# A two-layer hybrid step: small-block products of the scan in two rounds, layer norm chunk by chunk, tensor work from GpSimd to VectorE

## The chip, the core and the metric

One core of a Trainium2 chip. The metric is the device time of one execution in microseconds (us). Before the change the median of three runs is 2641.58 us (2641.39 to 2647.34). The profiler took one more execution, which is the one all rows below come from.

## What is computed

One step of a two-layer network on 256 tokens of width 2048: 128 prompt tokens (called g = 0 in the kernel) and 128 sample tokens (g = 1). Cut to the parts around the change:

```python
def hybrid_layer(x, mods, ...):          # once for prompt, once for sample; 2 layers
    shift1, scale1, gate1, shift2, scale2, gate2 = mods      # silu(c) @ w_mod + b_mod
    h = x * (1 + scale1) + shift1
    q, k, v, hq, hff, hfb, hi, hgt = split_in(h @ w_in)      # 2048 x 6656
    att = rms_norm(attend(q, k, v, sink), attn_g)
    hg, s_f, s_b = hgrn_mixer(hq, hff, hfb, hi, hgt, ...)    # two scans, forward and backward
    mix = concatenate([att, hg], -1) @ w_o
    x = layer_norm(ALPHA * x + gate1 * mix, ln_g[0], ln_b[0])
    ffn = square(relu((x * (1 + scale2) + shift2) @ w_up)) @ w_down   # 2048 x 8192 x 2048
    x = layer_norm(ALPHA * x + gate2 * ffn, ln_g[1], ln_b[1])

def hgrn_chunk_scan(q, k, v, log_f, s0):     # chunks of 32 tokens, 8 heads
    # inside a chunk: a = tril(q~ k~^T), o = a v
    # across chunks: s <- exp(sum log_f) * s + u;  o += (q exp(b)) s
```

## The kernel before

**Weights.** All large weights (w_in, w_o, w_up, w_down and the modulation weights w_mod) come from HBM as half tiles of 128x1024 (512 KB) into ten buffers `raw`, issued on SyncE's queue whenever a buffer is free. A 512x512 piece of a large weight is a main item. Its two halves are split into a rounded part `wh` (cast on ScalarE, L1324) and a rest `wl` (subtraction on VectorE, L1325), four buffers each, which is one main item ahead of TensorE. The activations are split in the same way (`hh`, `hl` and the like: L408 on ScalarE, L409 on VectorE). There are 392 main items. In a unit of kind T the weights are the stationary operand and the 256 tokens stream (48 matmuls of 256 columns: L436, L438, L439). In a unit of kind N the tokens are stationary and the weights stream (24 matmuls of 512 columns: L448, L449, L450), into one accumulator `acc` for each of the two groups of tokens; there are three such PSUM banks. Each item runs its k in two halves, both groups of tokens in each half.

**Modulation.** A piece of w_mod goes either to TensorE as 2-column matmuls into `psm` (L203, L223: the stationary operand is 2 columns wide, in a narrow column tile of the array) or to VectorE (`ma`, L266).

**Tasks around the mains.** Scans, attention, stores and the tail of a layer norm are generators; `between()` and a step after each main item advance them by up to a yield. So what a generator emits between two yields lands together in the stream of an engine. GpSimd and SyncE run in program order, TensorE, VectorE and ScalarE in the order that a scheduler makes of the program.

**The scan.** For two heads and both groups of tokens (m = 0..3) a scan works on four chunks of 32 tokens. The products inside a chunk go to `pI` (L748). The products across chunks go to `pX` in three rounds, one per later chunk: 4 matmuls with all 128 columns of `kd` stationary and 32 columns of `qb` streaming (L777), between them VectorE multiplies the earlier chunks of `kd` by decays; then a masked copy with masks `fx`, `bx` on VectorE takes `pX` over into `aT`. There are 16 such scans, eight per layer.

**End of a unit and of a stage.** A finished accumulator is taken over by VectorE: in w_o by `add_gated` (L887 multiplies by the gate, L890 or L892 adds to `Y`), in w_down by L1236 (adds to `Z`) or, in the last round, L1240 and L1241. The gate tiles `G` (128x512, two buffers) are loaded from DRAM by GpSimd's queue (L876) and the same two buffers serve the layer norm's scale and shift rows (L998, L999). `pre_sum` (L1224, L1225) multiplies `Z` by the gate.

**Layer norm.** After the last unit of w_o (and of w_down in the first layer) `ln_head` normalises all eight 128x512 tiles on VectorE (L909), then `ln_mod` transposes four chunks n by TensorE (L931), applies scale and shift (g = 0: two VectorE operations over 128x512, L934 and L936; g = 1: four ScalarE operations, L940) and splits. `ln_out` applies the norm's own scale and shift for the residual (L1002, L1003 on GpSimd) and runs as a task beside the next stage's mains.

## Time and profile before

| | us |
|---|---|
| median of 3 runs | 2641.58 |
| the profiled execution, its own time | 2641.68 |
| its span in the trace | 2639.9 |
| TensorE busy | 2536.6 (96%) |
| VectorE busy | 1862.5 (71%) |
| ScalarE busy | 1214.5 (46%) |
| GpSimd busy | 230.9 (9%) |
| mean rate of all transfers | 247 GB/s |

TensorE's busy time is a modelled one: matmuls overlap, and each record ends later than the next one starts. So 96% does not say that 4% is left; what TensorE loses is read from the distance of one start to the next, and from the waits. The stages by time: first layer's w_in to about 500, its w_o to 617, its MLP to about 1400, second layer's w_in to about 1800, its w_o to 1880, its MLP to 2618, and the last layer norm's tail to the end.

### The profile page before, as it was taken

The numbers are of one execution on the slowest core, as the hardware profiler recorded it, in microseconds if no ns is written. First come the engines' busy times: TensorE is split into PE (matmuls) and PEld (weight loads), VectorE is DVE, ScalarE is ACT, GpSimd is POOL, SyncE is SP. The second block draws the span as 40 slices with busy tenths as digits, with TensorE's granted clock in tenths as the row PEclk, the third lists the DMA queues.
The fourth block names the chain that finished last, engine by engine and source line by source line (L and its number), as shares of the span: only waits on it lengthen the run. The fifth ranks groups of instructions, "written<-read, shape, count | busy, mean of one in ns | idle before, by whom it ended". The sixth has DMA issues, their size and how long they took to land.

```text
span 2639.9 us, 41114 instructions
## 1 busy us (share of the span) xinstructions
PE 2536.6 (96%) x16276; PEld 2178.1 (83%) x16276; DVE 1862.5 (71%) x2290; ACT 1214.5 (46%) x1655; POOL 230.9 (9%) x266
## 2 busy tenths in 40 slices
PE   7999999998999999999999999999799999999996
PEld 4787777756988979979887989888798998998985
DVE  3455777658887777887778888877865565656656
ACT  3434554434444533534434656644454454443442
POOL 2000000014100000000014100001420000000003
PEclk9999999999999999999999999999899999999998
DMA  9889778868887878787879556566566666666663
GB/s 359 287 283 324 265 244 273 297 231 323 281 307 276 276 261 287 265 281 258 287 251 331 195 191 204 177 228 212 186 225 208 222 202 227 212 207 225 205 206 115
DMA packets 192369, 652.91 MB, mean 247 GB/s; under 512 B 22752, under 2 KB 25376, under 8 KB 192176
## 3 DMA queue, kind: packets, MB, share of 16 engines
q1 hardware_dynamic: 177680, 614.56, 68.0%
q0 software_dynamic: 11552, 33.04, 4.4%
q8 instruction: 127, 2.08, 0.3%
q10 hardware_dynamic: 2944, 2.69, 0.3%
q14 instruction: 66, 0.54, 0.1%
HBM read 643.32 MB, written 6.88 MB: 246 GB/s over the span
## 4 chain that ended last, share of the span: by engine, by line
PE 76%; DMA 10%; DVE 9%; issue 3%; ACT 1%; SPq 0%; POOL 0%; DVEq 0%; ACTq 0%; POOLq 0%
PE acc L436 12%; PE acc L439 12%; PE acc L438 12%; PE acc L448 11%; PE acc L449 11%; PE acc L450 11%; DMA raw<-in_w_mod_dram 6%; DVE wl L1325 3%; DVE ma L266 2%; PE psm L203 2%; PE pX L777 1%; DMA raw<-in_w_up_dram 1%; DMA raw<-in_w_in_dram 1%; PE psm L223 1%; DMA out_nsf_dram<-lf 1%
## 5 line engine op out<-in xcount | busy, mean ns | idle before, releaser
L1324 ACT CAST wh<-raw 128x1024 fp32r<-128x1024 f32 x784 | 821.8, 1049 | 1140.3 <-PE acc L450 489.0
L1325 DVE TENSOR_TENSOR wl<-raw,wh 128x1024 fp32r<-128x1024 f32 x784 | 971.2, 1246 | 433.3 <-ACT wh L1324 406.6
L436 PE MATMUL acc<-hh,wh 128*128 128x256 f32 x3072 | 875.9, 285 | 3.4 <-DVE q L599 1.9
L439 PE MATMUL acc<-hh,wl 128*128 128x256 f32 x3072 | 870.5, 284 | 7.9 <-DVE wl L1325 7.7
L438 PE MATMUL acc<-hl,wh 128*128 128x256 f32 x3072 | 869.7, 283 | 1.2 <-DVE hl L409 1.2
L436 PEld LDWEIGHTS acc<-hh,wh 128*128 128x128 f32 x3072 | 589.0, 192 | 39.2 <-issue 26.0
L439 PEld LDWEIGHTS acc<-hh,wl 128*128 128x128 f32 x3072 | 588.6, 192 | 11.2 <-DVE wl L1325 10.4
L438 PEld LDWEIGHTS acc<-hl,wh 128*128 128x128 f32 x3072 | 589.0, 192 | 2.9 <-DVE hl L409 2.2
L266 DVE SCALAR_TENSOR_TENSOR ma<-raw,stat,ma 128x1024 f32<-128x1024 f32 x300 | 388.5, 1313 | 113.4 <-DMA raw<-in_w_mod_dram 111.8
L448 PE MATMUL acc<-wh,fh 128*128 128x512 f32 x1024 | 401.8, 392 | 7.0 <-DVE Z L1236 6.8
L449 PE MATMUL acc<-wl,fh 128*128 128x512 f32 x1024 | 400.4, 391 | 0.4 <-DVE wl L1325 0.4
L450 PE MATMUL acc<-wh,fl 128*128 128x512 f32 x1024 | 399.7, 390 | 0.0
L448 PEld LDWEIGHTS acc<-wh,fh 128*128 128x128 f32 x1024 | 193.0, 188 | 57.8 <-DVE Z L1236 8.1
L449 PEld LDWEIGHTS acc<-wl,fh 128*128 128x128 f32 x1024 | 193.0, 188 | 40.8 <-DVE wl L1325 1.5
L450 PEld LDWEIGHTS acc<-wh,fl 128*128 128x128 f32 x1024 | 193.1, 189 | 40.4
L448 PE MATMUL acc<-wh,hh 128*128 128x512 f32 x320 | 129.5, 406 | 3.0 <-ACT hh L408 2.4
L449 PE MATMUL acc<-wl,hh 128*128 128x512 f32 x320 | 127.5, 398 | 0.3 <-DVE wl L1325 0.3
L450 PE MATMUL acc<-wh,hl 128*128 128x512 f32 x320 | 125.9, 394 | 1.9 <-DVE hl L409 1.9
L448 PE MATMUL acc<-wh,mxh 128*128 128x512 f32 x256 | 105.0, 411 | 5.9 <-DVE G L887 5.3
L876 POOL DMA_DIRECT2D G<-gr x48 | 26.3, 548 | 953.2 <-DVE Z L1241 408.9
L203 PE MATMUL psm<-raw,stat 128*2 128x512 f32 x640 | 96.6, 598 | 8.1 <-DMA raw<-in_w_mod_dram 8.1
L450 PE MATMUL acc<-wh,mxl 128*128 128x512 f32 x256 | 101.5, 398 | 0.0
(366 smaller groups left out, 2124.6 us busy)
## 6 DMA issues: line engine op xcount, KB each, us to landing
raw<-in_w_mod_dram SPq DMA_DIRECT2D x384, 512.0 KB
raw<-in_w_up_dram SPq DMA_DIRECT2D x256, 512.0 KB
raw<-in_w_down_dram SPq DMA_DIRECT2D x256, 512.0 KB
raw<-in_w_in_dram SPq DMA_DIRECT2D x208, 512.0 KB
raw<-in_w_o_dram SPq DMA_DIRECT2D x64, 512.0 KB
G<-gr POOLq DMA_DIRECT2D x48, 256.0 KB, 5.1
G<-in_lng_dram POOLq DMA_DIRECT2D x12, 256.0 KB, 5.8
G<-in_lnb_dram POOLq DMA_DIRECT2D x12, 256.0 KB, 7.1
```

The source lines that it names most:

```text
L203: pe.matmul(self.ps[32 * j:32 * j + 2, :], lhsT=stat[:, k, :], rhs=raw[j // 2][:, 512 * (j % 2):512 * (j % 2) + 512], start=k == 0, stop=k ...
L223: pe.matmul(self.ps[32 * j:32 * j + 2, :], lhsT=stat[:, 4 * k + j, :], rhs=raw[j // 2][:, 512 * (j % 2):512 * (j % 2) + 512], start=k == 0 ...
L266: dve.scalar_tensor_tensor(self.acc[g], raw[h], c, self.acc[g], ALU.mult, ALU.add)
L436: pe.matmul(ps, lhsT=w0, rhs=hi[:, k], start=f and k == 0 and m % 2 == 0, stop=False, skip_group_check=True)
L438: pe.matmul(ps, lhsT=w0, rhs=lo[:, k], start=False, stop=False, skip_group_check=True)
L439: pe.matmul(ps, lhsT=w1, rhs=hi[:, k], start=False, stop=e and k == 3 and m % 2 == 1, skip_group_check=True)
L448: pe.matmul(ps, lhsT=hi[:, k, gs], rhs=wh[k], start=f and k == 0, stop=False)
L449: pe.matmul(ps, lhsT=hi[:, k, gs], rhs=wl[k], start=False, stop=False)
L450: pe.matmul(ps, lhsT=lo[:, k, gs], rhs=wh[k], start=False, stop=e and k == 3)
L777: pe.matmul(pX[:, 128 * m + 32 * c:128 * m + 32 * c + 32], lhsT=kd[:, 128 * m:128 * m + 128], rhs=qb[:, 128 * m + 32 * c:128 * m + 32 * c ...
L1324: act.copy(wh, r)
L1325: dve.tensor_tensor(wl, r, wh.bitcast(F32), ALU.subtract)
```

## The change

1. In the last item of each N unit, the 12 matmuls of g = 0 come first, then `between()`, then those of g = 1 (`n_tile`).
2. The scan's products across chunks take two rounds: first two blocks of 32x32 for each m (8 matmuls, 32 stationary columns), then one of 64x64 (4 matmuls, 64 stationary columns), each at the column tile of the array where its rows lie. Three ScalarE copies take them over; the masks `fx` and `bx`, their loads and casts go.
3. `ln_head` goes; `ln_mod` normalises two tiles for each chunk n, then transposes, g = 1 first. `scale_shift` does g = 0 by four VectorE operations over 128x128; the first layer's input uses it too.
4. The additions of `add_gated` (12), the multiplications of `pre_sum` (16) and both operations of `ln_out` (48) move from GpSimd to VectorE: 76 operations over 128x512.
5. `ln_out` is spread by yields: 24 ahead of it, 6 behind each pair of loads, 3 behind each tile.

```diff
-        for key in ("fi", "bi", "fx", "bx"):
+        for key in ("fi", "bi"):
...
+        if un.kind == "N" and e:
+            for g in range(2):
+                if g == 1:
+                    between()
+                n_tile(un, g, range(4), hi, lo, wh, wl, f, e)
+            return
...
+    def n_tile(un, g, ks, hi, lo, wh, wl, f, e):
+        if f and ks[0] == 0:
+            un.ps[g] = accp.tile([128, 512], F32, tag="acc", name=nm("acc"))
+        ps = un.ps[g]
+        gs = slice(128 * g, 128 * g + 128)
+        for k in ks:
+            pe.matmul(ps, lhsT=hi[:, k, gs], rhs=wh[k], start=f and k == 0, stop=False)
+            pe.matmul(ps, lhsT=hi[:, k, gs], rhs=wl[k], start=False, stop=False)
+            pe.matmul(ps, lhsT=lo[:, k, gs], rhs=wh[k], start=False, stop=e and k == 3)
...
-        order = [0, 1, 2, 3] if fwd else [3, 2, 1, 0]
+        c0, c1, c2, c3 = order = [0, 1, 2, 3] if fwd else [3, 2, 1, 0]
+
+        early, late = slice(min(c0, c1), max(c0, c1) + 1), slice(min(c2, c3), max(c2, c3) + 1)
+        cols = lambda m, sl: slice(128 * m + 32 * sl.start, 128 * m + 32 * sl.stop)
+        rows = lambda sl: slice(32 * sl.start, 32 * sl.stop)
+        one = lambda c: slice(c, c + 1)
         pX = bank("pX")
+
+        def across(ss, ts):
+            for m in range(4):
+                pe.matmul(pX[rows(ss), cols(m, ts)], lhsT=kd[:, cols(m, ss)], rhs=qb[:, cols(m, ts)],
+                          start=True, stop=True, tile_position=(0, 32 * ss.start))
+
+        across(one(c0), one(c1))
+        across(one(c2), one(c3))
...
-        for i in range(1, 4):
-            c = order[i]
-            pc = order[:i]
-            if i >= 2:
-                sl = slice(min(pc[:-1]), max(pc[:-1]) + 1)
-                n = i - 1
-                d = dm[:, :, pc[-1]:pc[-1] + 1].unsqueeze(3).to_broadcast([128, 4, n, 32])
-                kk = kdv[:, :, sl, :]
-                flat = lambda x: x.rearrange("p m c t -> p m (c t)")
-                dve.tensor_tensor(flat(kk), flat(kk),
-                                  dm[:, :, pc[-1]:pc[-1] + 1].to_broadcast([128, 4, n * 32]), ALU.mult)
-            for m in range(4):
-                pe.matmul(pX[:, 128 * m + 32 * c:128 * m + 32 * c + 32], lhsT=kd[:, 128 * m:128 * m + 128],
-                          rhs=qb[:, 128 * m + 32 * c:128 * m + 32 * c + 32], start=True, stop=True)
-            if i == 1:
-                cum = small(8).rearrange("p (h c) -> p h c", h=2)
-                for hl in range(2):
-                    m = 2 * hl + 1
-                    dve.memset(cum[:, hl, order[0]:order[0] + 1], 1.0)
-                    for x in range(1, 4):
-                        pcol, ccol = order[x - 1], order[x]
-                        dve.tensor_tensor(cum[:, hl, ccol:ccol + 1], cum[:, hl, pcol:pcol + 1],
-                                          dm[:, m, pcol:pcol + 1], ALU.mult)
-                for hl in range(2):
-                    dve.tensor_tensor(
-                        qS[:, 128 * hl:128 * hl + 128].rearrange("p (c t) -> p c t", c=4),
-                        qbv[:, 2 * hl + 1], cum[:, hl, :].unsqueeze(2).to_broadcast([128, 4, 32]), ALU.mult)
-            yield
-        cs = slice(32 * min(order[1:]), 32 * max(order[1:]) + 32)
-        dve.copy_predicated(v3(aT, 4)[:, :, cs],
-                            masks[mk + "x"][:, cs].unsqueeze(1).to_broadcast([128, 4, 96]),
-                            v3(pX, 4)[:, :, cs])
-        pc = order[:3]
-        lc = order[3]
-        for m in (0, 2):
-            sl = slice(128 * m + 32 * min(pc), 128 * m + 32 * max(pc) + 32)
-            dve.tensor_scalar(kd[:, sl], kd[:, sl], dm[:, m, lc:lc + 1], None, ALU.mult)
+        cum = small(8).rearrange("p (h c) -> p h c", h=2)
+        do = dm[:, 1::2]
+        dve.memset(cum[:, :, c0:c0 + 1], 1.0)
+        for x in range(1, 4):
+            pc, cc = order[x - 1], order[x]
+            dve.tensor_tensor(cum[:, :, cc:cc + 1], cum[:, :, pc:pc + 1], do[:, :, pc:pc + 1], ALU.mult)
+        for hl in range(2):
+            dve.tensor_tensor(qS[:, 128 * hl:128 * hl + 128].rearrange("p (c t) -> p c t", c=4),
+                              qbv[:, 2 * hl + 1], cum[:, hl, :].unsqueeze(2).to_broadcast([128, 4, 32]), ALU.mult)
+        yield
+        dve.tensor_tensor(kdv[:, :, c0], kdv[:, :, c0], dm[:, :, c1:c1 + 1].to_broadcast([128, 4, 32]), ALU.mult)
+        dve.tensor_tensor(qbv[:, :, c3], qbv[:, :, c3], dm[:, :, c2:c2 + 1].to_broadcast([128, 4, 32]), ALU.mult)
+        across(early, late)
+        yield
+        aTv = v3(aT, 4)
+        for ss, ts in ((one(c0), one(c1)), (one(c2), one(c3)), (early, late)):
+            act.copy(aTv[rows(ss), :, rows(ts)], v3(pX, 4)[rows(ss), :, rows(ts)])
+
+        de = small(2).unsqueeze(2)
+        dg = dm[:, 0::2]
+        kg = kdv[:, 0::2]
+        dve.tensor_tensor(de, dg[:, :, c2:c2 + 1], dg[:, :, c3:c3 + 1], ALU.mult)
+        flat = lambda x: x.rearrange("p m c t -> p m (c t)")
+        dve.tensor_tensor(flat(kg[:, :, early]), flat(kg[:, :, early]), de.to_broadcast([128, 2, 64]), ALU.mult)
+        dve.tensor_tensor(kg[:, :, c2], kg[:, :, c2], dg[:, :, c3:c3 + 1].to_broadcast([128, 2, 32]), ALU.mult)
...
-            (dve if n == 3 else pool).tensor_tensor(y, y, t, ALU.add)
+            dve.tensor_tensor(y, y, t, ALU.add)
...
-    def ln_head(key):
-        mr = ln_stat(key)
-        for n in range(4):
-            for g in range(2):
-                y = yt[key, n, g]
-                dve.tensor_scalar(y, y, mr[g][0], mr[g][1], ALU.subtract, ALU.mult)
...
+    def scale_shift(out, src, A, B, g):
+
+        for c in range(4):
+            o_, s_ = (x[:, 128 * c:128 * c + 128] for x in (out, src))
+            if g == 0:
+                dve.tensor_scalar(o_, s_, A[:, c, g:g + 1], B[:, c, g:g + 1], ALU.mult, ALU.add)
+            else:
+                act.activation(o_, s_, AF.Identity, scale=A[:, c, g:g + 1], bias=B[:, c, g:g + 1])
+
     def ln_mod(key, AB, dst):
 
         A, B = AB
+        mr = ln_stat(key)
         for n in range(4):
             hl = new_act("h")
-            for g in range(2):
+            fs = slice(4 * n, 4 * n + 4)
+            for g in (1, 0):
+                y = yt[key, n, g]
+                dve.tensor_scalar(y, y, mr[g][0], mr[g][1], ALU.subtract, ALU.mult)
+            for g in (1, 0):
                 y = yt[key, n, g]
                 pt = bank("pt")
                 for c in range(4):
                     pe.transpose(pt[:, 128 * c:128 * c + 128], y[:, 128 * c:128 * c + 128], K["ident"])
                 t = u("ed")
-                if g == 0:
-                    dve.tensor_tensor(v3(t, 4), v3(pt, 4),
-                                      A[:, 4 * n:4 * n + 4, g:g + 1].to_broadcast([128, 4, 128]), ALU.mult)
-                    dve.tensor_tensor(v3(t, 4), v3(t, 4),
-                                      B[:, 4 * n:4 * n + 4, g:g + 1].to_broadcast([128, 4, 128]), ALU.add)
-                else:
-                    for c in range(4):
-                        act.activation(t[:, 128 * c:128 * c + 128], pt[:, 128 * c:128 * c + 128], AF.Identity,
-                                       scale=A[:, 4 * n + c, g:g + 1], bias=B[:, 4 * n + c, g:g + 1])
+                scale_shift(t, pt, A[:, fs], B[:, fs], g)
...
-        tag = "G"
+        for _ in range(24):
+            yield
         for n in range(4):
-            gt, bt = u(tag), u(tag)
+            gt, bt = u("G"), u("G")
             side.dma_start(gt, a["lng"][li:li + 1, 512 * n:512 * n + 512].partition_broadcast(128))
             side.dma_start(bt, a["lnb"][li:li + 1, 512 * n:512 * n + 512].partition_broadcast(128))
+            for _ in range(6):
+                yield
             for g in range(2):
                 y = yt.pop((key, n, g))
-                pool.tensor_tensor(y, y, gt, ALU.mult)
-                pool.tensor_tensor(y, y, bt, ALU.add)
+                dve.tensor_tensor(y, y, gt, ALU.mult)
+                dve.tensor_tensor(y, y, bt, ALU.add)
                 sink_fn(n, g, y)
-            yield
+                for _ in range(3):
+                    yield
...
-                    pool.tensor_tensor(t, t, gch[l, 5, n, g, 0], ALU.mult)
+                    dve.tensor_tensor(t, t, gch[l, 5, n, g, 0], ALU.mult)
```

In the changed kernel the lines are shifted: L777 is L780, L448 to L450 are L457 to L459, L1236 is L1241, L1325 is L1329, `ln_out`'s operations are L1013 and L1014.

The order of instructions on TensorE at the first layer's first two scans, before (`t` and `ed` are the scan's `kd` and `qb`):

```order
L450 MATMUL acc_2698<-wh_2686,hl_2037 128x512
L448 MATMUL acc_2705<-wh_2686,hh_2036 128x512
L777 MATMUL pX_2642<-t_2489,ed_2532 128x32 x4
L777 MATMUL pX_2662<-t_2498,ed_2544 128x32 x4
L449 MATMUL acc_2705<-wl_2687,hh_2036 128x512
L450 MATMUL acc_2705<-wh_2686,hl_2037 128x512
L777 MATMUL pX_2642<-t_2489,ed_2532 128x32 x4
L777 MATMUL pX_2662<-t_2498,ed_2544 128x32 x4
```

And after, the first round of the first scan:

```order
L458 MATMUL acc_2698<-wl_2563,hh_2020 128x512
L459 MATMUL acc_2698<-wh_2562,hl_2021 128x512
L780 MATMUL pX_2642<-t_2489,ed_2532 32x32 x8
L457 MATMUL acc_2705<-wh_2562,hh_2020 128x512
L458 MATMUL acc_2705<-wl_2563,hh_2020 128x512
```

and its second round, at the same weights as before (`wh_2686`, and the item's second half `wh_2690`):

```order
L458 MATMUL acc_2698<-wl_2687,hh_2034 128x512
L459 MATMUL acc_2698<-wh_2686,hl_2035 128x512
L457 MATMUL acc_2698<-wh_2690,hh_2034 128x512
L458 MATMUL acc_2698<-wl_2691,hh_2034 128x512
L459 MATMUL acc_2698<-wh_2690,hl_2035 128x512
L780 MATMUL pX_2642<-t_2489,ed_2532 64x64 x4
L780 MATMUL pX_2662<-t_2498,ed_2544 64x64 x4
L457 MATMUL acc_2698<-wh_2690,hh_2034 128x512
L458 MATMUL acc_2698<-wl_2691,hh_2034 128x512
```

Three rounds of `128x32 x4` for each scan have become one `32x32 x8` and one `64x64 x4`. The last rows also show the new order in a unit's last item: `acc_2698` goes on to the second half of the weights, where before `acc_2705` had its turn.

On VectorE, at the end of a w_down unit in the first MLP, before (`Z` is the running sum over units, `ma` the modulation sum):

```order
L266 SCALAR_TENSOR_TENSOR ma_9071<-raw_9369,stat,ma_9071 128x1024
L266 SCALAR_TENSOR_TENSOR ma_9072<-raw_9369,stat,ma_9072 128x1024
L1236 TENSOR_TENSOR Z_7610<-Z_7610,acc_9257 128x512
L1236 TENSOR_TENSOR Z_7612<-Z_7612,acc_9264 128x512
L1325 TENSOR_TENSOR wl_9410<-raw_9299,wh_9409 128x1024
```

And after, at the end of the same unit (the tiles' numbers are shifted, 7610 to 7614):

```order
L1329 TENSOR_TENSOR wl_9384<-raw_9263,wh_9383 128x1024
L1241 TENSOR_TENSOR Z_7614<-Z_7614,acc_9265 128x512
L266 SCALAR_TENSOR_TENSOR ma_9079<-raw_9377,stat,ma_9079 128x1024
L266 SCALAR_TENSOR_TENSOR ma_9080<-raw_9377,stat,ma_9080 128x1024
L1241 TENSOR_TENSOR Z_7616<-Z_7616,acc_9272 128x512
L1329 TENSOR_TENSOR wl_9418<-raw_9307,wh_9417 128x1024
```

The two additions that free the accumulators stood together behind the modulation's operations; now they stand apart, the first directly behind the split `wl`.

On GpSimd, at the start of the second layer's MLP, before:

```order
L998 DMA G_18015<-in_lng_dram 128x512
L999 DMA G_18016<-in_lnb_dram 128x512
L1002 TENSOR_TENSOR Y_17008<-Y_17008,G_18015 128x512
L1003 TENSOR_TENSOR Y_17008<-Y_17008,G_18016 128x512
L1002 TENSOR_TENSOR Y_17012<-Y_17012,G_18015 128x512
L1003 TENSOR_TENSOR Y_17012<-Y_17012,G_18016 128x512
L998 DMA G_18061<-in_lng_dram 128x512
L999 DMA G_18062<-in_lnb_dram 128x512
```

And on VectorE in the changed kernel, for the same tiles `Y`:

```order
L409 TENSOR_TENSOR hl_18012<-ed_18032,hh_18011 128x4x128
L1013 TENSOR_TENSOR Y_17024<-Y_17024,G_18819 128x512
L1013 TENSOR_TENSOR Y_17028<-Y_17028,G_18819 128x512
L1329 TENSOR_TENSOR wl_18176<-raw_17839,wh_18175 128x1024
L1014 TENSOR_TENSOR Y_17024<-Y_17024,G_18820 128x512
L1014 TENSOR_TENSOR Y_17028<-Y_17028,G_18820 128x512
L1013 TENSOR_TENSOR Y_17151<-Y_17151,G_19163 128x512
L1329 TENSOR_TENSOR wl_18232<-raw_17875,wh_18231 128x1024
L1013 TENSOR_TENSOR Y_17155<-Y_17155,G_19163 128x512
L1014 TENSOR_TENSOR Y_17151<-Y_17151,G_19164 128x512
L1329 TENSOR_TENSOR wl_18236<-raw_17877,wh_18235 128x1024
L1014 TENSOR_TENSOR Y_17155<-Y_17155,G_19164 128x512
```

GpSimd waited by itself for the reloads of `G` between these operations; now they stand in VectorE's stream, between the splits `wl`, and the second pair of loads (`G_19163`, `G_19164`) uses the buffers of the first (`G_18819`, `G_18820`).

## Rows read from the trace of the kernel before

**Rows 1.** The page, part 1: busy us (share of the span) and instructions of each engine.

```profile
PE 2536.6 (96%) x16276; PEld 2178.1 (83%) x16276; DVE 1862.5 (71%) x2290; ACT 1214.5 (46%) x1655; POOL 230.9 (9%) x266
```

**Rows 2.** Windows: length, busy PE, PEld, DVE, ACT, POOL, PEclk, DMA share, GB/s.

```profile
254.00:500.00 246.00, 236.71 (x1623) 186.04 (x1616) 183.57 (x371) 123.70 (x227) 14.83 (x28) 0.99 0.77 261
...
620.00:1390.00 770.00, 754.58 (x4817) 664.39 (x4816) 617.87 (x566) 352.62 (x402) 52.65 (x46) 1.00 0.81 277
...
1420.00:1850.00 430.00, 420.18 (x2841) 379.60 (x2840) 342.36 (x552) 239.24 (x400) 47.19 (x62) 1.00 0.63 208
...
1930.00:2618.00 688.00, 687.52 (x4358) 625.33 (x4358) 412.08 (x377) 309.14 (x341) 22.61 (x31) 1.00 0.63 208
```

**Rows 3.** Single lines: duration ns min/median/max, first and last start, form.

```profile
L777 PEld LDWEIGHTS pX<-t,ed x192: 187/192/192, 279.7 to 1651.6; 128*128 128x128 f32 x192
L777 PE MATMUL pX<-t,ed x192: 190/276/276, 279.9 to 1651.6; 128*128 128x32 f32 x192
L275 PEld LDWEIGHTS ph<-ma,ones x80: 106/108/109, 740.3 to 2529.9; 128*32 128x32 f32 x80
```

**Rows 4.** Timeline: start us, us from first start to last end, record, count.

```profile
30.88 1.05 PE L233 MATMUL pt<-sel,w 128*128 128x2 f32 x8 [0.69 <-ACT w L230]
...
289.12 1.87 PE L777 MATMUL pX<-t,ed 128*128 128x32 f32 x16
```

**Rows 5.** Timeline at a change from 128 stationary columns to 2 and back.

```profile
929.14 0.39 PE L450 MATMUL acc<-wh,fl 128*128 128x512 f32 x1
929.46 1.04 PE L203 MATMUL psm<-raw,stat 128*2 128x512 f32 x8
930.43 0.50 PE L448 MATMUL acc<-wh,fh 128*128 128x512 f32 x1
```

**Rows 6.** Waits of TensorE: us in total, times, longest.

```profile
PE pI L748 <- DVE e L742: 9.7, 7, 2.4
...
PE acc L439 <- DVE wl L1325: 7.7, 9, 1.6
...
PE acc L448 <- DVE Z L1236: 6.8, 3, 2.4
PE acc L448 <- DVE G L887: 5.3, 2, 3.5
```

**Rows 7.** Timeline at the end of a w_down unit.

```profile
939.10 1.28 DVE L1236 TENSOR_TENSOR Z<-Z,acc 128x512 f32<-128x512 f32 x2
...
939.83 0.50 PE L448 MATMUL acc<-wh,fh 128*128 128x512 f32 x1 [2.23 <-DVE Z L1236]
```

**Rows 8.** A window of TensorE alone behind it: busy, PEclk, DMA share, GB/s.

```profile
940.90:944.30 3.40, 3.40 (x10) 0.51 0.97 339
```

**Rows 9.** Timeline of the layer norm behind the second layer's w_o.

```profile
1879.73 0.39 PE L450 MATMUL acc<-wh,mxl 128*128 128x512 f32 x1
...
1886.25 6.60 DVE L909 TENSOR_SCALAR Y<-Y,s,s 128x512 f32<-128x512 f32 x8
...
1886.94 3.29 PE L931 MATMUL pt<-ident,Y 128*128 128x128 f32 x16 [6.83 <-DVE Y L909]
...
1895.97 0.75 PE L436 MATMUL acc<-hh,wh 128*128 128x256 f32 x2
```

**Rows 10.** GpSimd's multiplications of `ln_out`, by line.

```profile
L1002 POOL TENSOR_TENSOR Y<-Y,G x16: 1268/1750/3134, 618.9 to 1925.4; 128x512 f32<-128x512 f32 x16
```

**Rows 11.** Timeline of VectorE beside them.

```profile
633.08 1.23 DVE L1325 TENSOR_TENSOR wl<-raw,wh 128x1024 fp32r<-128x1024 f32 x1
...
635.93 4.56 DVE L1325 TENSOR_TENSOR wl<-raw,wh 128x1024 fp32r<-128x1024 f32 x2
```

**Rows 12.** The page, part 6: loads into `G`, count, KB, us from issue to landing.

```profile
G<-in_lng_dram POOLq DMA_DIRECT2D x12, 256.0 KB, 5.8
G<-in_lnb_dram POOLq DMA_DIRECT2D x12, 256.0 KB, 7.1
```

**Rows 13.** Timeline at the start: a mask's cast waits for its load.

```profile
37.58 0.23 DVE L157 CAST mbi<-mbi 128x128 uint8<-128x128 int32 x1 [2.12 <-DMA mbi<-in_mbi_dram]
```

More of the change, by code (lines that the diff above doesn't have):

```diff
@@ L1068, in first_h @@
             x = xT[n][g]
[L1069 to L1075 removed]
+            scale_shift(x, x, s1, sh, g)
             split_act(hl, (slice(None), slice(0, 4), slice(128 * g, 128 * g + 128)), v3(x, 4))
```

51 lines of the change are left out of this document (16 added, 35 removed).

## The prediction

> **What bounds the kernel now.** I read the page's busy times first: TensorE is busy 96% of the span, VectorE 71%, ScalarE 46% [rows 1]. So TensorE's own work and its waits set the time, unless the weights come too late. The windows say where that could be [rows 2]: the second MLP has almost no idle time (687.52 of 688), the first MLP 15 us in 770, and both stages with scans about 10 us in 246 and in 430. The share of the transfers is 0.77 and 0.81 in the first layer, 0.63 in the second. So time saved on TensorE counts in full in the second layer; in the first it brings the weights' rate nearer to its limit, and I count it at 70% there (at 100% if the transfers had no limit, at nothing if they were the bound; TensorE's busy 236.71 of 246 is nearer to the former).
>
> So there are two places to save: work of TensorE that is not weights times tokens (`pX`), and waits.
>
> **Products across chunks.** 192 matmuls give 384 records, two forms of 192 (one is shown) [rows 3]. Sixteen records take 1.87 us [rows 4], 0.11 from one to the next, so 384 x 0.11 = 42 us. The stationary side sets this pace: a product with only 2 streaming columns but 128 stationary ones has about the same (eight in 1.05). Loading 128 columns takes 192 ns and 32 columns 108 [rows 3]; the difference is 84/96 = 0.87 ns a column, and 128 x 0.87 = 0.111 us is just that pace. By this slope 32 columns cost 0.028 and 64 cost 0.056. After: 16 scans x 8 x 2 records x 0.028 = 7.2, and 16 x 4 x 2 x 0.056 = 7.2, together 14.
>
> New is the change of the array's column tiling, into and out of 32 blocks. At 929.14 a matmul starts, and the 2-column one behind it 0.32 later instead of the steady 0.23: 0.09 to enter. Eight records of 0.107 end at 930.32, the next matmul starts at 930.43: 0.12 to leave [rows 5]. So 32 x 0.21 = 6.7. Gain: 42 - 14 - 7 = 21; half of it at 70%, **18**. Bounds: +28 if a change of tiling costs nothing, -7 if small blocks are no cheaper than large ones and the changes come on top.
>
> The Trainium skill, "TensorEngine Tiling (Array Packing)", section Key Properties, speaks against this edit: changing the tiling mode drains the engine. Were each of the 64 changes to wait for the end of the running matmul (0.39, where the next one normally starts after 0.23), that would be 0.16 x 64 = 10 instead of 7, and the term 15 instead of 18. The row has 0.09 and 0.12, so the drain is there but not whole; the measurement decides.
>
> The scan's VectorE work gets lighter (a masked copy and the multiplications of ever more chunks go), three small ScalarE copies come, hidden at ScalarE's 46%. TensorE waits 9.7 us in scans for VectorE's `e` [rows 6]; with one round fewer I take **+3** of it, between 0 and 10.
>
> **End of N units.** With three banks and two accumulators per unit, the next unit's second accumulator has to wait until VectorE has freed one. The list has 6.8 and 5.3 us for it [rows 6]; at 939.1 two additions of 0.64 stand behind other work, TensorE goes on at 939.83 after 2.23 idle [rows 7]. A wait of this length has a second price: behind it the granted clock is 0.51 for 3.4 us, thus the lower level, 1.2 GHz [rows 8], which loses half of 3.4; three such stretches lose 5. Together 17. After the change g = 0's accumulator is complete 12 x 0.227 = 2.7 us earlier, and its addition may run while g = 1 is still streaming. That covers four of the five waits (their mean is 2.2), and most of the longest, 3.5. I take **+13**, bounds 5 and 18 (VectorE takes its work in the scheduler's order, so an addition can again stand behind a split and two `ma`).
>
> **Layer norm.** Behind the second layer's w_o the last matmul starts at 1879.73 and the first of the MLP at 1895.97 [rows 9]. In between, all eight normalisations (6.60 us) stand ahead of the first chunk's scaling. After: the statistics are ready at 1886.25 as before; two normalisations take 1.65, then transposes of g = 0 (0.8), four small scalings and a split of 0.6 and 0.7: first matmul near 1889.7. Gain 6. The other two norms stand beside modulation weights that stream at the transfers' pace, so I give them 3 together. **+9**, bounds 4 and 12.
>
> **GpSimd to VectorE.** 76 operations of 0.64 (the price of [rows 7]'s additions) add 49 us to VectorE. GpSimd needed 1.75 for one [rows 10]. But VectorE is slower while GpSimd works: two splits take 4.56 where one takes 1.23 alone [rows 11]. So some of the 49 comes back (48 of these operations in `ln_out` alone), and VectorE at 71% has room. TensorE waits 7.7 us for `wl` [rows 6], mostly beside `ln_out`; I take **+5**, bounds 0 and 8.
>
> The price is in the `ln_out` of the second layer's MLP: by the order VectorE multiplies with `G_19163` only 2.6 us (a split of 1.23 and two operations of 0.64) behind the last use of that buffer, and a load needs 5.8 to 7.1 [rows 12] and an issue. So VectorE stands 3.5 to 5 us in front of each of the three later pairs, with a `wl` queued behind. The splits are one main item ahead, 24 x 0.227 = 5.4 us, which covers most of it; `pre_sum` has the same at six places with one main's lead. **-5**, bounds 0 and -30.
>
> **Start and tail.** At 37.58 a mask's cast waits 2.12 for its load [rows 13], ahead of a split. Two masks go, but by the order three operations on the lower-bound rows, whose load is issued behind this mask's, now stand in front of that split: **-2** (bounds 0, -3). The last norm's tail on VectorE instead of GpSimd: +0.5, as most of it waits for the final sums.
>
> **Sum.** 18 + 3 + 13 + 9 + 5 - 5 - 2 + 0.5 = 41.5. The profiled execution took 2641.68 (span 2639.9 and 1.8 around it), as good as the median 2641.58. Prediction: **2600**.
>
> **Rivals.**
> 1. Small blocks cost as much as large ones (a fixed price per matmul, or load and stream one behind the other). For: no row has 32 stationary columns with 32 streaming ones. Against: the slope of [rows 3]. The `pX` term goes from +18 to between -7 and +5: 2613 to 2625. Chance 0.15.
> 2. The weights take back what the first layer saves: of the sum some 27 lie there. For: shares of 0.77 to 0.81 as a mean, which hide stretches near 0.97 [rows 8]. Against: TensorE is busy 236.71 of 246 at 0.77 [rows 2], so the weights keep up there. Leaves 10 to 20 less: 2610 to 2620. Chance 0.10.
> 3. More comes: tile changes cheap, all waits for accumulators gone, the scans' waits too (+7 +5 +7 +3): 2570 to 2588. Chance 0.14.
> 4. VectorE's waits for reloads of `G` reach TensorE. For: the order. Against: the lead of one main. A load that lands L us after its issue (0.5) costs TensorE L + 0.5 - 2.6 - 5.4 = L - 7.5 at each of nine places. At 11 to 12.5 us instead of 5.8 to 7.1 that is 3.5 to 5 each, and the sum without my -5, 2595, becomes 2626 to 2640 (0.08). It decides against the change from some 13 us on, where nine times 5.5 outweighs the gain of 46; at 14 us it gives 2654 (0.05).
>
> The likeliest case, 2588 to 2612, has 0.48. The range 2574 to 2628 takes in rivals 1 and 2 and most of 3. What a measurement can tell from no change is 0.3%, 8 us: faster 0.91, same 0.04, slower 0.05.
>
> **What would show it.** `pX` records: 32-wide ones at 0.03, 64-wide at 0.06 from one to the next, and gaps of 0.1 around each block. At the ends of w_down units no wait for `Z` over 1 us and no window at half clock. From the last matmul of w_o to the first of the MLP about 10 us instead of 16.2. VectorE's splits at 1.23 throughout. At the second layer's MLP start VectorE waits of 3 to 5 us for `in_lng` and `in_lnb`, with less than 2 each on TensorE. The prediction is wrong if the small blocks run at 0.11, if new waits of `acc` for `wl` sum to over 10 us, or if the windows' transfer share reaches 0.95 in the first layer.

## The result, and the profile after

The changed kernel takes 2595.68 us (median of four, 2595.02 to 2602.27) where the kernel before takes 2641.48 beside it: 45.8 us less, a ratio of 0.9827 with a 95% interval of 0.9806 to 0.9848. The forecast was 2600. The sum was right; several of its terms were not, and the runs below say which.

The page's first part for the changed kernel (as [rows 1]):

```profile
PE 2508.7 (97%) x16276; PEld 2150.2 (83%) x16276; DVE 1849.1 (71%) x2332; ACT 1227.5 (47%) x1703; POOL 105.0 (4%) x188
```

TensorE is still the bound. VectorE took over 76 operations and is not busier than before (1849 us after 1862). Some of that comes from lighter scans, but the move made alone (a run below) also leaves it at 1857: what VectorE lost by the operations it got back by running undisturbed. The single lines show both this and the new products. First the split `wl`, min/median/max in ns, in the changed kernel:

```profile
L1329 DVE TENSOR_TENSOR wl<-raw,wh x784: 1161/1224/1230, 33.3 to 2562.4; 128x1024 fp32r<-128x1024 f32 x196
```

Not one of 784 splits takes over 1.23 us; before, two took 4.56 together [rows 11]. Then the products across chunks (one of two forms):

```profile
L780 PEld LDWEIGHTS pX<-t,ed x192: 106/113/139, 282.8 to 1614.0; 128*32 128x32 f32 x128, 128*64 128x64 f32 x64
L780 PE MATMUL pX<-t,ed x192: 195/197/270, 282.8 to 1614.0; 128*32 128x32 f32 x128, 128*64 128x64 f32 x64
```

and the timeline of one first round among matmuls of an N unit:

```profile
282.50 0.40 PE L459 MATMUL acc<-wh,hl 128*128 128x512 f32 x1
...
282.83 0.59 PE L780 MATMUL pX<-t,ed 128*32 128x32 f32 x16
...
283.35 0.49 PE L457 MATMUL acc<-wh,hh 128*128 128x512 f32 x1
```

Sixteen records of 32 stationary columns take 0.59 us from the first start to the last end, where sixteen of 128 columns took 1.87 [rows 4]. From one start to the next that is 0.026 us in the mean (0.031 by the median of all such pairs), and those of 64 columns follow each other by 0.058, the median (the sums had 0.028 and 0.056). The first starts 0.33 behind the last large matmul, not 0.227: 0.10 to enter.

What TensorE waits for now (us in total, times, longest):

```profile
PE acc L458 <- DVE wl L1329: 9.0, 6, 3.6
PE pI L757 <- DVE e L751: 8.1, 4, 6.1
PE pX L780 <- DVE ed L797: 7.2, 2, 5.4
PE pt L947 <- DVE Y L942: 6.7, 1, 6.7
...
PE pI L757 <- DVE lf L752: 2.2, 1, 2.2
...
PE acc L457 <- DVE Z L1241: 1.8, 1, 1.8
...
PE pO L818 <- ACT e L802: 1.0, 1, 1.0
PE acc L445 <- DVE Z L1241: 0.9, 1, 0.9
```

Against [rows 6], the waits for accumulators (6.8 for `Z` and 5.3 for w_o's `G`) are 1.8 and nothing; the last row's 0.9 was 0.7. The waits in the scans have grown: 8.1 and 7.2, each with one long wait, and two smaller rows make 18.5, where the kernel before has 12.8 (9.7 and 3.1). And there are new waits for splits, the longest 3.6.

To see where the 46.5 us of span were gained, I counted main items by their matmuls in the trace (48 of 256 columns or 24 of 512 for each) and took the time from one item's start to another's. "Again" is a second profile of the changed kernel; the last four columns are the changed kernel with one part put back, told of below. The items left out differ by about 1 us at most.

| items | what runs there | before | changed | again | scan back | order back | norm back | GpSimd back |
|---|---|---|---|---|---|---|---|---|
| 0 to 8 | start | 53.9 | 56.8 | 56.9 | 56.8 | 55.4 | 56.9 | 55.3 |
| 32 to 54.5 | scans, layer 1 | 222.7 | 213.6 | 213.0 | 221.4 | 212.9 | 214.2 | 213.8 |
| 59.5 to 61 | last attention, modulation | 36.0 | 28.1 | 28.4 | 28.3 | 36.9 | 28.2 | 28.1 |
| 61 to 67.5 | w_o | 44.2 | 40.4 | 40.4 | 40.4 | 40.5 | 40.4 | 42.8 |
| 67.5 to 69 | first norm | 27.3 | 22.2 | 24.1 | 23.6 | 23.8 | 23.3 | 29.1 |
| 69 to 77 | MLP start | 52.0 | 47.3 | 47.3 | 47.3 | 47.3 | 47.2 | 50.7 |
| 77 to 184 | MLP | 639.2 | 632.3 | 632.8 | 633.5 | 638.8 | 630.3 | 635.3 |
| 184 to 200 | MLP end, second norm | 106.1 | 108.8 | 109.7 | 107.1 | 109.1 | 107.8 | 102.9 |
| 200 to 250 | w_in and scans, layer 2 | 357.9 | 351.8 | 353.9 | 360.0 | 353.2 | 351.8 | 356.7 |
| 262 to 264 | w_o end, third norm | 32.3 | 22.3 | 22.6 | 22.2 | 23.0 | 23.6 | 27.6 |
| 264 to 274 | MLP start | 60.3 | 62.3 | 63.5 | 63.5 | 62.2 | 63.6 | 63.1 |
| | span | 2639.9 | 2593.4 | 2600.8 | 2611.1 | 2611.3 | 2594.7 | 2612.6 |

Two profiles of the same kernel agree within 2.1 us in each of these stages, though their spans differ by 7.4. So a stage tells more than a time, and, going by this one pair, differences of about 2 in a stage mean nothing.

The largest surprise is the third row: 8 us at the first layer's last attention, in no term of the forecast.

### The profile page after: what moved, and what is told of

The parts are those of the page before. It is cut to its first block, busy times and chain, and to the rows that moved or that the text cites. A ratio compares the mean times of both kernels' runs of the same rounds, so it can differ in the third digit from the quotient of the medians.

```text
span 2593.4 us, 41149 instructions
## 1 busy us (share of the span) xinstructions
PE 2508.7 (97%) x16276; PEld 2150.2 (83%) x16276; DVE 1849.1 (71%) x2332; ACT 1227.5 (47%) x1703; POOL 105.0 (4%) x188
## 4 chain that ended last, share of the span: by engine, by line
PE 61%; issue 28%; DMA 5%; DVE 4%; ACT 1%; POOL 0%; SPq 0%; POOLq 0%; DVEq 0%; ACTq 0%
PE acc L445 9%; PE acc L447 9%; PE acc L448 9%; PE acc L457 9%; PE acc L459 9%; PE acc L458 9%; DMA raw<-in_w_mod_dram 2%; PE psm L203 2%; DVE wl L1329 1%; PE psm L223 1%; DMA out_nsf_dram<-lf 1%; PE pI L757 1%; PE pX L780 1%; DMA raw<-in_w_in_dram 0%; PE pO L818 0%
## 5 line engine op out<-in xcount | busy, mean ns | idle before, releaser
L1329 DVE TENSOR_TENSOR wl<-raw,wh 128x1024 fp32r<-128x1024 f32 x784 | 953.6, 1222 | 416.1 <-ACT wh L1328 397.1
L448 PE MATMUL acc<-hh,wl 128*128 128x256 f32 x3072 | 871.3, 284 | 5.5 <-DVE wl L1329 5.5
L448 PEld LDWEIGHTS acc<-hh,wl 128*128 128x128 f32 x3072 | 589.9, 192 | 6.5 <-DVE wl L1329 6.5
L266 DVE SCALAR_TENSOR_TENSOR ma<-raw,stat,ma 128x1024 f32<-128x1024 f32 x300 | 378.6, 1281 | 95.0 <-DMA raw<-in_w_mod_dram 91.2
L457 PE MATMUL acc<-wh,fh 128*128 128x512 f32 x1024 | 400.6, 391 | 1.8 <-DVE Z L1241 1.8
L459 PE MATMUL acc<-wh,fl 128*128 128x512 f32 x1024 | 398.9, 390 | 0.0
L457 PEld LDWEIGHTS acc<-wh,fh 128*128 128x128 f32 x1024 | 192.3, 188 | 51.0 <-issue 7.7
L459 PEld LDWEIGHTS acc<-wh,fl 128*128 128x128 f32 x1024 | 192.3, 188 | 40.0
L457 PE MATMUL acc<-wh,hh 128*128 128x512 f32 x320 | 131.3, 412 | 2.1 <-ACT hh L408 2.1
L459 PE MATMUL acc<-wh,hl 128*128 128x512 f32 x320 | 127.8, 402 | 0.0
L457 PE MATMUL acc<-wh,mxh 128*128 128x512 f32 x256 | 103.2, 404 | 0.0
L458 PE MATMUL acc<-wl,mxh 128*128 128x512 f32 x256 | 100.1, 392 | 0.0
L459 PE MATMUL acc<-wh,mxl 128*128 128x512 f32 x256 | 100.0, 392 | 0.0
```

The lines of the kernel that those rows point to most:

```text
L266: dve.scalar_tensor_tensor(self.acc[g], raw[h], c, self.acc[g], ALU.mult, ALU.add)
L448: pe.matmul(ps, lhsT=w1, rhs=hi[:, k], start=False, stop=e and k == 3 and m % 2 == 1, skip_group_check=True)
L457: pe.matmul(ps, lhsT=hi[:, k, gs], rhs=wh[k], start=f and k == 0, stop=False)
L458: pe.matmul(ps, lhsT=hi[:, k, gs], rhs=wl[k], start=False, stop=False)
L459: pe.matmul(ps, lhsT=lo[:, k, gs], rhs=wh[k], start=False, stop=e and k == 3)
L1329: dve.tensor_tensor(wl, r, wh.bitcast(F32), ALU.subtract)
```

## The experiments

**The scan's products put back** (the changed kernel, three rounds and masks of before):

```diff
-        across(one(c0), one(c1))
-        across(one(c2), one(c3))
...
+        for i in range(1, 4):
...
+                pe.matmul(pX[:, 128 * m + 32 * c:128 * m + 32 * c + 32], lhsT=kd[:, 128 * m:128 * m + 128],
+                          rhs=qb[:, 128 * m + 32 * c:128 * m + 32 * c + 32], start=True, stop=True)
```

> The changed kernel with the scan's products as before (three rounds of 128 stationary columns, masked copies, the two masks loaded again); everything else changed. Theory: the narrow blocks are worth 40 us of records against 22, so 18, less what the masks cost at the start: 2611 to 2616 where the changed kernel has 2595.7. Rival 1: the narrow blocks bring nothing because the scans' waits eat them: 2594 to 2600. Rival 2: they are worth more than their records, because the wait at the first layer's last attention (8 us gained there, not forecast) comes from them too: 2619 to 2624.

Median 2608.43 (2603.88 to 2612.89), ratio to the kernel before 0.9839 (0.9806 to 0.9872). By time this cannot be told from the changed kernel's 0.9827: the theory's 2611 to 2616 would be a ratio of 0.9884 to 0.9903, above the interval, and the ratio lies in rival 1's range (0.982 to 0.9843). By stages it can: the two stages with scans are longer by 7.8 and 8.2, the others agree within 2.1. That is near the theory's 18; nothing came back at the attention, so rival 2 is out. The stages speak against rival 1, the time for it: the profiled execution is the longest of four (2612.89, the shortest 2603.88), and how much of the 16 us the other executions lose is not shown.

**The order in a unit's last item put back** (both groups of tokens in each half):

```diff
-        if un.kind == "N" and e:
-            for g in range(2):
-                if g == 1:
-                    between()
-                n_tile(un, g, range(4), hi, lo, wh, wl, f, e)
-            return
```

> The changed kernel with both groups of tokens in each half of a unit's last item again, as before. Theory: the waits for accumulators at the ends of N units come back, with their stretches at half clock: 13 to 17 us, 2609 to 2613. Rival: the waits were those of a VectorE slowed by GpSimd and do not come back, since that work has moved: 2594 to 2600.

2615.82 (2613.12 to 2619.57), 0.9873 (0.9847 to 0.9899). The theory's size, but half of it elsewhere: 8.8 at the last attention, 6.5 in the first MLP; behind the second layer's w_o less than 1 comes back. So this order is what the 8 us hang on. TensorE's waits for `Z` are 6.0 and 1.6 again, those for w_o's `G`, 5.3 before, only 0.3: they are also gone where only the GpSimd operations were moved (a run below), so either edit removes them. The traces show how the order reaches the attention. VectorE at that place in the kernel before, and the next products of the attention on TensorE:

```profile
525.82 0.69 DVE L504 TENSOR_REDUCE s<-ps 128x4 f32<-128x512 f32 x1 [3.64 <-PE ps L530]
527.25 1.23 DVE L1325 TENSOR_TENSOR wl<-raw,wh 128x1024 fp32r<-128x1024 f32 x1 [0.74 <-ACT wh L1324]
528.39 0.68 DVE L887 TENSOR_TENSOR G<-acc,G 128x512 f32<-128x512 f32 x1
528.99 0.15 DVE L506 SCALAR_TENSOR_TENSOR s<-s,sink 128x4 f32<-128x4 f32 x1
...
541.52 0.70 PE L565 MATMUL ps<-kx,q 128*128 128x256 f32 x2
```

and in the changed kernel:

```profile
518.91 0.69 DVE L896 TENSOR_TENSOR G<-acc,G 128x512 f32<-128x512 f32 x1 [2.75 <-PE acc L459]
519.63 0.69 DVE L899 SCALAR_TENSOR_TENSOR Y<-Y,G 128x512 f32<-128x512 f32 x1
520.24 0.68 DVE L513 TENSOR_REDUCE s<-ps 128x4 f32<-128x512 f32 x1
520.96 0.16 DVE L515 SCALAR_TENSOR_TENSOR s<-s,sink 128x4 f32<-128x4 f32 x1
...
529.92 0.48 PE L574 MATMUL ps<-kx,q 128*128 128x256 f32 x1 [0.29 <-DVE q L570]
```

The softmax of the attention is a chain of small operations on VectorE, ScalarE and TensorE. Before, its second step (L506) stood behind a split that waited for its cast and behind the unit's gating (L887), which waits for the accumulator's last matmul: 3.2 us from the first step to the second. Now g = 0's accumulator is ready early, the gating stands ahead of the chain, and the steps follow by 0.7. These two steps give 2.5 us; from the first step to the next products of the attention it is 15.7 us before and 9.7 now. Which of the later waits of that stretch (2.44 us for modulation weights, 1.91 for an exponential, in the trace before) follow from this and which from the transfers, I have not separated.

**The norm put back** (all eight normalisations first, two operations for g = 0's scale and shift):

```diff
-            for g in (1, 0):
-                y = yt[key, n, g]
-                dve.tensor_scalar(y, y, mr[g][0], mr[g][1], ALU.subtract, ALU.mult)
...
+            put_call(lambda: ln_head(k1))
```

> The changed kernel with all eight normalisations ahead of the first transposes, scale and shift of the prompt's half in two operations, as before; the first layer's input keeps the new form. Theory: the chunk-by-chunk norm is worth 5 at each of the two norms behind w_o and 1 at the third: 2604 to 2608. Rival: only the norm behind the second layer's w_o counts, the others stand beside transfers: 2599 to 2602.

2597.15 (2592.75 to 2600.37), 0.9801 (0.9775 to 0.9827). Theory and rival both fall: nothing is lost that can be measured, and the norm's stages are within 1.4 of the changed kernel's. VectorE and TensorE at the third norm in this run:

```profile
1841.66 3.74 DVE L918 TENSOR_SCALAR Y<-Y,s,s 128x512 f32<-128x512 f32 x8
1845.31 1.29 DVE L952 TENSOR_TENSOR ed<-pt,A 128x512 f32<-128x512 f32 x2
...
1847.91 0.51 PE L445 MATMUL acc<-hh,wh 128*128 128x256 f32 x2 [0.15 <-ACT hh L408]
```

and in the changed kernel:

```profile
1836.41 0.39 PE L459 MATMUL acc<-wh,mxl 128*128 128x512 f32 x1
...
1842.82 2.83 DVE L942 TENSOR_SCALAR Y<-Y,s,s 128x512 f32<-128x512 f32 x6
1843.51 4.18 PE L947 MATMUL pt<-ident,Y 128*128 128x128 f32 x24 [6.71 <-DVE Y L942]
...
1848.06 0.51 PE L445 MATMUL acc<-hh,wh 128*128 128x256 f32 x2 [0.36 <-ACT hh L408]
```

The eight normalisations that took 6.60 us in the kernel before [rows 9] take 3.74 in the same order: they were slow because GpSimd's `ln_out` ran beside them, not because there were eight. Its first multiplication started at 1888.12, and in the trace of the kernel before the five normalisations ahead of that take 0.54 each and the three behind it 1.48 to 1.50. The first layer's norm in that same trace has eight undisturbed ones:

```profile
613.11 3.74 DVE L909 TENSOR_SCALAR Y<-Y,s,s 128x512 f32<-128x512 f32 x8
```

From the first normalisation to the first matmul it is 6.25 in the old order (1841.66 to 1847.91) and 5.24 in the new (1842.82 to 1848.06): the chunk-by-chunk order is worth 1 us here. From the last matmul of w_o to the first of the MLP it is 16.24 before, 11.65 in the changed kernel, 12.71 in this run and 15.39 in the next one, which has the new order and GpSimd beside it.

**The 76 operations put back on GpSimd:**

```diff
-                dve.tensor_tensor(y, y, gt, ALU.mult)
-                dve.tensor_tensor(y, y, bt, ALU.add)
+                pool.tensor_tensor(y, y, gt, ALU.mult)
+                pool.tensor_tensor(y, y, bt, ALU.add)
```

> The changed kernel with the 76 operations on GpSimd again, spread by the new yields. Theory: VectorE is slowed beside GpSimd, but its waits of 3 to 5 us for the loads of G go away; the two were forecast at 5 each: 2593 to 2600, and splits of 2.2 us beside GpSimd's multiplications appear again while the waits of TensorE for splits behind G loads (at 1298, 1879, 1897 us) vanish. Rival: the move is the main gain, since a slowed VectorE also delays the release of weight buffers and thus the transfers of the first layer: 2604 to 2615.

2614.09 (2604.47 to 2617.51), 0.986 (0.9829 to 0.9891). The rival's size is right; the theory's range (up to a ratio of 0.9843) only touches the end of the interval. The stages say where: first norm +6.9, MLP start +3.4, w_o +2.4, MLP +3.0, layer 2's w_in +4.9, the end of w_o with the third norm +5.3; only the end of the first MLP is shorter (5.9), without waits for loads of `G` in VectorE's stream. VectorE at the first MLP's start in this run:

```profile
626.50 3.46 DVE L1329 TENSOR_TENSOR wl<-raw,wh 128x1024 fp32r<-128x1024 f32 x2
629.88 2.33 DVE L266 SCALAR_TENSOR_TENSOR ma<-raw,stat,ma 128x1024 f32<-128x1024 f32 x1
632.13 2.31 DVE L1329 TENSOR_TENSOR wl<-raw,wh 128x1024 fp32r<-128x1024 f32 x1
```

1.22 and 1.28 become 2.3. That VectorE is slow beside GpSimd is shown; the rival's own mechanism, that this delays the weights, is not.

**The same kernel again**, as a measure for the three runs beside it.

> The changed kernel itself, unaltered, as a measure for the three beside it: 0.9827 of the kernel before (2595.7 of 2641.5), and the times of its stages as in its first profile within 1 us each. If the stages differ by more, the differences of a few us between variants mean nothing.

2600.02 (2594.87 to 2613.42), 0.9834 (0.9803 to 0.9865). The ratio repeats; the stages do so within 2.1 instead of 1.

**The scan's state stored from another tile.** The long waits in the scans lead to this row of VectorE's waits in the changed kernel, its timeline, and TensorE behind it:

```profile
DVE lf L703 <- DMA out_nsf_dram<-lf: 19.7, 7, 5.2
```

```profile
312.79 0.15 DVE L703 TENSOR_SCALAR lf<-Y 128x1 f32<-128x1 f32 x1 [5.17 <-DMA out_nsf_dram<-lf]
...
322.24 0.98 PE L757 MATMUL pI<-e,lf 128*128 128x128 f32 x3 [6.15 <-DVE e L751]
```

In the last part of this wait and behind it, the granted clock is at the lower level, 1.2 GHz (TensorE's window: length, busy, PEclk, DMA share, GB/s):

```profile
320.60:327.40 6.80, 5.16 (x17) 0.50 0.09 19
```

A scan stores its final state to DRAM from half of its tile `lf`; of these there are two, so the next but one scan cannot begin until the store has been done. The edit takes the tile of the start state for it, which nothing reads any more:

```diff
-        act.copy(kN[:, 256:512], pF[:, 0:256])
+        act.copy(s0, pF[:, 0:256])
...
-        back.dma_start(dst[l, :, 128 * h0:128 * h0 + 256], kN[:, 256:512])
+        back.dma_start(dst[l, :, 128 * h0:128 * h0 + 256], s0)
```

> The changed kernel, with the scan's final state stored from the tile of its start state instead of from half of lf, so that no later scan waits for that store before it may write lf. Theory: VectorE's 19.7 us of waits for that store (7 times, up to 5.2) hold the next scan back and reach TensorE as 6.1 us at 316 and 5.4 us at 1513: 8 to 14 us less than the changed kernel, the two stages with scans shorter by 4 to 7 each. Rival: the scans wait for other things then (their own chain of VectorE and ScalarE operations): within 3 us of the changed kernel.

2579.81 (2572.55 to 2581.59), 0.9752 (0.9736 to 0.9769): 20 us less than the changed kernel on the same chip, more than the theory had. The first layer's scans take 198.0 instead of 213.0, the second layer's 349.2 instead of 353.9. VectorE's row for the store is gone, TensorE's waits in the scans fall from 18.5 to 4.6, and in the first layer's scans no stretch at the lower clock is left: the wait was paid a second time by the clock behind it.

**Five buffers for gate and norm rows during the MLPs**, and gate rows loaded a unit earlier. VectorE in the changed kernel at the first MLP's last units:

```profile
1293.25 0.68 DVE L1245 TENSOR_TENSOR G<-acc,G 128x512 f32<-128x512 f32 x1
1298.27 0.69 DVE L1229 TENSOR_TENSOR Z<-Z,G 128x512 f32<-128x512 f32 x1 [4.34 <-DMA G<-gr]
```

and at the second layer's MLP start:

```profile
1867.35 0.69 DVE L1013 TENSOR_TENSOR Y<-Y,G 128x512 f32<-128x512 f32 x1 [2.72 <-DMA G<-in_lng_dram]
...
1876.70 0.69 DVE L1013 TENSOR_TENSOR Y<-Y,G 128x512 f32<-128x512 f32 x1 [4.58 <-DMA G<-in_lng_dram]
```

```diff
-        t = u("G")
+        t = u("e1" if v == 5 and g == 0 else "G")
...
-            gt, bt = u("G"), u("G")
+            gt, bt = u("G"), u("G" if li % 2 else "e1")
...
+                    if n < 3:
+                        put_call(pre_gate(5, n + 1, 0))
```

> The changed kernel, with five buffers in place of two for the gate rows and the norm's rows during the MLPs (tiles that only scans and attention use elsewhere), and the gate rows loaded one unit earlier. Theory: VectorE's waits for loads of G (14.4 us for the gate, 10.1 for the norm) are what makes TensorE wait for splits at 1298, 1879 and 1897 us: 6 to 9 us less than the changed kernel, 4 of it in the last units of the first MLP and 3 at the start of the second. Rival: those waits come from modulation weights that VectorE waits for in its order (as at 1200 and 1216 us): within 2 us of the changed kernel.

2589.51 (2586.79 to 2595.88), 0.979 (0.9772 to 0.9809): 10.5 us less by the medians, and the intervals just overlap. The stages: items 184 to 200 take 101.4 instead of 109.7, items 264 to 274 take 58.9 instead of 63.5, and the MLP before (77 to 184) is 2.7 longer. At the second layer's MLP start VectorE's waits for the norm's rows fall from 11 to 1.3. In the first MLP's last units its waits for gate rows stay:

```profile
1305.64 0.69 DVE L1229 TENSOR_TENSOR Z<-Z,G 128x512 f32<-128x512 f32 x1 [4.27 <-DMA G<-gr]
1325.80 0.69 DVE L1229 TENSOR_TENSOR Z<-Z,G 128x512 f32<-128x512 f32 x1 [4.09 <-DMA G<-gr]
```

Yet TensorE's waits for splits in that stage fall from 5.7 to 2.1, and the item that held the longest of them, 3.6, takes 5.4 us instead of 9.3: the waits are as long, but this one no longer reaches TensorE. By the medians the edit is worth some 10 us, and the loads cost the changed kernel up to that: some 3.5 us of what the stage gained lies at other items, and their cause is not shown.

**Both edits:**

> Both of these edits. Theory: they lie in different stages and add: 14 to 22 us less than the changed kernel, some 2574 to 2582 where the kernel before takes 2641.5. Rival: the first layer's share is taken back by the transfers, and only the second layer's counts: 6 to 10 us less.

2573.95 (2572.91 to 2577.59), 0.9731 (0.9716 to 0.9745), 26 us less than the changed kernel beside it, 72 less than the kernel before. The gains add, but for 5 us: the first MLP (77 to 184) is 5.3 longer than in the changed kernel, as it was 2.7 longer in the run before, though not with the store's edit alone. The traces show where. In the changed kernel TensorE waits 1.84 for `Z` at 1100.2 (2.3 in the second profile), and the granted clock stays at 1.00 through this MLP. Here it waits 2.70 at the same unit's end and 2.76 for a split at 1195.4, and behind each the clock is at the lower level:

```profile
1090.90:1094.30 3.40, 3.40 (x8) 0.50 0.96 306
1196.70:1200.10 3.40, 3.40 (x18) 0.50 0.84 320
```

The two items concerned make up 4.9 of the 5.3. Why the waits are longer is open.

**Each part alone, in the kernel before.** The same edits as in the diff, one at a time.

> The kernel before with the scan's new products alone (and the two masks gone). Theory: what was undone alone gave 16 us in the two stages with scans, 8 in each; done alone it should give the same, less 2.5 at the start: 2624 to 2630 where the kernel before takes 2641.5. Rival: the scans of the kernel before hang on their waits (for the state's store, for VectorE beside GpSimd), so shorter products alone give under 6 us.

2635.64 (2629.62 to 2640.89) beside 2645.32 of the kernel before, 0.9956 (0.9939 to 0.9972): 11.6 us by the ratio. That is the low end of the theory's range (2624 to 2630, ratios up to 0.9956), and the rival's under 6 us is out. The stages with scans give 9.2 and 9.7, of which 4.8 are lost again in the first MLP and 4.0 at the second's start.

> The kernel before with the new order in a unit's last item alone. Theory: the eight us at the first layer's last attention and most of the waits at the ends of N units (6.5 in the first MLP, 4 behind the second layer's w_o) go: 2622 to 2630. Rival: the attention's eight us need VectorE's other changes as well: 2630 to 2636.

2624.83 (2620.14 to 2630.04), 0.9922 (0.9904 to 0.9939): 20.6 us. The attention's stretch takes 28.7 instead of 36.0, with no other part of the change; the rival is out. The first MLP gains 3.2, where the theory had 6.5, w_o 2.3 and the third norm's stretch 1.3; layer 2's w_in and scans lose 3.9. The profiled execution is the longest of four, and its span is only 11.6 below that of the kernel before, so the stages place about half of the 20.6.

> The kernel before with the 76 operations on VectorE alone, without the new yields, all normalisations still first. Theory: the norms and the starts of the MLPs gain what they lost when GpSimd got the work back (6 at the first norm, 3 behind it, 5 at the norm of the second layer, 5 in the second layer's w_in): 2620 to 2628. Rival: without the yields the norm's operations stand in VectorE's way right behind the norm, with the loads of G in front of them: 2636 or more.

2635.15 (2631.28 to 2635.69), 0.9956 (0.9939 to 0.9973): 11.6 us, between the two and nearer the theory (0.9919 to 0.9949 as ratios; the rival from 0.9979). Both mechanisms are in it: w_o gains 3.7, the norm behind it 3.5, the third norm with the end of w_o 8.7; but without the yields the end of the first MLP with the second norm loses 7.6, the first MLP's start 2.4 and layer 2's w_in 4.0.

> The kernel before with the scan's final state stored from the tile of its start state. Theory: the store's wait was in the kernel before as well (VectorE waited 18 us for it, up to 3.7 at once) and was worth as much there: 2620 to 2630, with the stages with scans shorter by 7 to 15 and 4 to 8. Rival: it was hidden there behind the longer products and only came out with the change: 2636 to 2642.

2632.71 (2627.93 to 2641.43), 0.9956 (0.9939 to 0.9972): 11.6 us in a kernel where nothing else is changed, at the edge of the theory's range, and the rival is out. So the store's wait stood in the kernel before as well. The scans' stages give 13.6 and 3.0 (the theory had 7 to 15 and 4 to 8), where the changed kernel has 15.0 and 4.7. By time the removal is worth nearly twice as much in the changed kernel; by these stages it is nearly the same, and the kernel before loses it again elsewhere, 4.6 in the first MLP, 4.6 at the second's start and 3.8 at the attention. The profiled execution is the longest of six and not shorter than that of the kernel before.

## Why the prediction was right

**Small products: the mechanism and the price right.** 42 us of records were forecast to become 14 with 7 for the changes of tiling. By the starts of all records they are 40 and 22, changes of tiling included (0.09 to enter, 0.10 to leave, from the median distances, against 0.09 and 0.12). That is 18, and the two stages with scans give 16 when the old products are put back and 19 when the new ones are made alone. By the whole time it is 11.6 made alone, because 9 were lost again elsewhere, and only 1 to 3 put back. Rival 1 (narrow blocks as dear as wide ones) is refuted by the pace alone. By the drain rule (the Trainium skill, "TensorEngine Tiling (Array Packing)", Key Properties) a change of tiling costs; the trace agrees, with some 0.1 us each way, which is less than waiting for a whole matmul's end. The +3 for the scans' waits was wrong: these waits were not VectorE's work but the state's store, which no step of the forecast saw; TensorE's waits in the scans rose by 5.7 instead of falling by 3, and the store cost 20 us of the changed kernel. The share of the transfers is 0.79 in the first layer's scans and 0.82 in its MLP, so nothing shows the weights taking the gain back as rival 2 had it.

**Ends of N units: too small.** +13 was forecast (the five waits that it counts have a mean of 2.4, not 2.2), 20.6 measured alone; put back, it costs 10 to 12 by the ratios and 18 by the stages. Some 7 is at the places that were seen: waits for accumulators, and stretches at the lower clock behind them, of which the changed kernel's trace has none between 327 and 1382 us. One wait of 1.8 for `Z` is left, where none over 1 was expected. 7 to 9 came from the attention, where the same edit takes VectorE's gating out of the way of a softmax. The term looked at who waits for the accumulator, not at what stands behind the operation that empties it.

**Layer norm: the wrong cause.** +9 was forecast and about 1 is due to the order. The row of 6.60 us [rows 9] was read as eight operations of 0.83 in line; alone the eight take 3.74, and the rest was GpSimd beside the last three. The two that the forecast put ahead of the first transposes at 1.65 took 1.0 already before the change. From the first normalisation to the first matmul the sum had 3.5; it is 5.24, and 11.65 from w_o's last matmul, where about 10 was expected. The first norm's stage became shorter by 5.1 and the distance from w_o's last matmul to the MLP in the second layer by 4.6, but mostly by the next part.

**GpSimd to VectorE: too small.** +5 for contention and -5 for loads of `G` were to cancel. Done alone it gives 11.6. Put back, it costs 7 to 9 by the ratios; by the stages, 26 are lost in six of them and 6 gained in one. The contention was taken only where TensorE waited for `wl`; it also lengthened norms and gating. The Trainium skill, "SBUF — State Buffer", section "Who interferes with whom", has a lock on a shared port pair that only one of the two engines can hold, against a VectorE operation with two inputs in SBUF such as the split; the rows agree as far as a split beside a GpSimd operation takes 2.3 us and never does so in the changed kernel, where GpSimd has none of the 76 (1230 ns at most).

**Loads of G: the mechanism right, the price too low.** VectorE stands 2.7 to 4.6 us in front of loads, at the places named. At the second layer's MLP start TensorE waits 1.1 and 1.5 behind them, under 2 as forecast; in the first MLP's last units it is 3.6. TensorE's share is up to 10 us by the run with five buffers, not 5 (rival 4's mechanism, far from the point where it decides). The new waits for splits sum to 6 us (14.5 after 8.3), under the 10 that would have spoken against the forecast.

**Start.** -2 was forecast: item 8 comes 2.6 later than before. The size is right, the cause is not shown: with the masks back the stretch still takes 56.8 us, and with the scan's new products and no masks in the kernel before 54.3 instead of 53.9.

**The sum.** The three parts made alone give 11.6, 20.6 and 11.6, together 43.8, and the norm's order about 1: they add up to nearly all of the 45.8, each with some 4.5 us of uncertainty. Put back one at a time they cost 1 to 3, 10 to 12 and 7 to 9, some 20 together. So the parts overlap (the waits for `G` go with either of two), or the ratios put back, uncertain by 7 to 9 each, are too low; that is open, and the addition is no proof. The forecast came near it because its errors have both signs: the norm 8 too much, the scans (18 and 3, less 2 at the start) 7 too much, the unit ends 8 too little and GpSimd's move, with the loads of `G`, 12 too little. A right sum was in part luck.

## What to carry to other kernels

A row that is long may be long because of its neighbour: compare its mean with the same form where the other engine rests, before one prices a reordering of it. Look at stores too: a tile that is the source of a store keeps its buffer until the store is done, and with two buffers the next but one user waits; here that cost 11.6 us in one kernel and 20 in the faster one. And when an edit lets an operation run earlier, ask what stands behind it on its engine: at the attention that was worth as much as the wait which one saw.
